# Two streams for a step's preparation in a single-core RWKV-7 and short-convolution layer

## The chip, the cores and the metric

The kernel runs on one core of a Trainium2 chip. The metric is the device time of one execution in microseconds; the time given for a kernel is the median of several runs. The profile shows one execution.

## What is computed

One layer of a hybrid encoder on 1024 prompt tokens (one sequence) and 128 sample tokens (8 sequences of 16), D_MODEL 1024, 16 heads of 64. In short:

```python
h = rmsnorm(x, g_norm)
proj = h @ w_in                       # [r, k, v, w_lr, a_lr, z_a | B, C, xb, z_b | g_a, g_b]
pa_mix = pa + mu_shift * (pa_prev - pa)
r, k, v, w_lr, a_lr, z_a = split(pa_mix)
w = exp(-DECAY_SCALE * sigmoid(w_decay0 + tanh(w_lr) @ w_decay2))
a = sigmoid(w_iclr0 + a_lr @ w_iclr2)
kt = k * (1 + (a - 1) * k_replace)
kh = (k * k_removal) / norm(k * k_removal)            # per head
# per token: S = S*diag(w) - (S kh)(a*kh)^T + v kt^T ;  y = S r
o_a = (groupnorm(y) + sum(r * kt * r_bonus) * v) * silu(z_a)
out_b = (B * conv3(C * xb) * silu(z_b)) @ w_o_b
x = x + (sigmoid(g_a) * (o_a @ w_o_a) + sigmoid(g_b) * out_b) @ w_out
x = x + sigmoid(rmsnorm(x, g_ple) @ w_ple_gate) * (p @ w_ple)
y = rmsnorm(x, g_final)
```

## The kernel before, in words

The features lie on the 128 partitions, the tokens along the free dimension. A projection of one 128-column tile of w_in over a block of n tokens is 8 x 3 = 24 matmuls with float16 high and low parts (`dense_parts`, line 162); it accumulates in one of the two PSUM buffers of the pool psd. The tokens go in three blocks: 512 prompt tokens, the 128 sample tokens, the other 512 prompt tokens (BLOCKS, line 22).

The recurrence is done in 24 **steps**: 8 pairs of heads (j) times the three blocks (g); i counts them. A step passes through generators, called streams:

- `prep` (line 364): the decay and the learning rate (`decay`, line 376: products lod and loa, a scan, exponentials), then in one loop the projections of k, r, v and z (TensorE's dk, dr, dv, dz), each mixed with the token before (`mixed`, line 221). After r come the norm of the keys (product pss, a reciprocal square root on VectorE, the broadcast rnb on ScalarE), after v the transposes prn and the scaled keys, after z its tanh (thz) and silu. Ahead of v it waits until the tail of step i-3 is done (line 411), as v and z have three buffers. Temporary tiles come from a pool of seven slots ("ta", TA on line 241).
- `keys` (line 466), the end of prep: the scaled keys and receptances ar and kb. It waits until the step before has transposed its kb (line 470), and at first until all three openings are done.
- `scores` (line 496, psc), `values` (line 525: pk, pv, psb, x), `inverse` (line 568: itt, ig, i, ie, if), a triangular inverse by doubling.
- `chain` (line 656): the recurrence over chunks of 64 tokens, one after another, 8 chunks in a 512-token step and 2 in the sample step; products c and u, state sbd.
- `tail` (line 710): the output y, its group norm on VectorE, transposes py, and the gating with z.

Beside them run `opening` (line 300: normalised input of a block and the low-rank input projection), `conv` (line 781: the four projections C, x, zb and B of the convolution branch for 8 tiles) and `gates_b` (line 832), which computes up to six tiles of the merge gates early (EARLY, line 209: gates b0 to b3, a6 and a7) and stores them in memory (gb_d).

The order of TensorE's work is written out when the program is built, by `go` (line 916), with a clock of modelled TensorE time. A `yield` of a number says how much modelled time the next part needs until its inputs are there. What is ready and no projection goes first, in the order of the list of streams (line 903). Otherwise the next three matmuls of a projection are issued: one that has begun goes on to its end, else a new one begins, the convolution's first where it is behind its pace (its share of its work against the share of chunks done), else by the order of the list:

```python
            fills = more or [x for x in live if x.next == DENSE]
            if fills:
                behind = S_conv.cost / CONV_US < (chunks[0] + LEAD) / 144
                fills.sort(key=lambda x: (x is S_conv) != behind)
                fills[0].step()
```

The table `may` (line 905 on) says when a stream may take its next step. The early gates start when the convolution is done, and none starts when all tails are done (line 913). Weights come in over SP's queue (`load_q`, line 334), in the third step of a pair those of the next pair, and are split by ScalarE and VectorE. The other engines' order is set by a planner from priorities and data.

After the steps the kernel computes the gates that were not early, the two output projections (ob, oa), the merge and w_out (oc), and the per-layer input embedding (pg, ple) with the norms.

Of the kernel before, what the change touches and what calls it, by code (L numbers as in the profile page):

```python
# [23 lines left out]
RN = 512  # L24
# [47 lines left out]
def _build(nc, tc, I, O, top):  # L72
# [40 lines left out]
    def P(n, i):  # L113
        o, w = PN[n]
        return par[:, o + i:o + i + 1]
# [102 lines left out]
    def tt(pool, tag, nm, bufs, n=RBUF):  # L218
        return pool.tile([128, n], F32, tag=tag, name=nm, bufs=bufs)
# [21 lines left out]
    TA = 7  # L241
# [86 lines left out]
    def pair(j):  # L328
        if j not in pairs:
            pairs[j] = s = St()  # L330
            s.w, s.lora = {}, False
        return pairs[j]

    def load_q(j, q):
        s = pair(j)
        if q not in s.w:
            t = {"k": T_K, "r": T_R, "v": T_V, "z": T_ZA}[q]
            s.w[q] = load_w(I["w_in"][t + j], f"p{j}_{t}")
# [25 lines left out]
    def prep(f):  # L364

        j, g = f.j, f.g
        f.s = s = pair(j)
        load_lora(j)
        if g == 0:
            s.sst = wk.tile([128, 8, 64], F32, tag="sst", name=f"sst{j}", bufs=1)  # L370
            SP.dma_start(s.sst, I["wkv"][j])
        blk = o, n = f.blk
        smp, nch, npr, nm = f.smp, f.nch, f.npr, f.nm
        sl, ns = (16, 8) if smp else (64, nch)

        def decay():
            th = []
            yield lambda: f.i or S_open.at > 0
            for q, hb in (("d", 0), ("a", 1)):
                yield 2.0 * hb  # L380
                ps = psa.tile([128, 512], F32, tag="a", name="lo" + q + nm)
                lr = (lrd, lra)[hb]
                mm(ps[:, :n], s.lwh[:, hb, :], lr[:, o:o + n], start=True, stop=False)
                mm(ps[:, :n], s.lwl[:, hb, :], lr[:, o:o + n], start=False, stop=True)
                t = tt(st_, "ta", "th" + q + nm, TA)[:, :n]
                A.activation(t, ps[:, :n], AF.Tanh, scale=0.5 * IWS, bias=half[:, hb, j:j + 1])
                th.append(t)
            thd, tha = th
            G.tensor_scalar(out=thd, in0=thd, scalar1=1.0, scalar2=None, op0=ALU.add)
            cum = tt(st_, "ta", "cum" + nm, TA)[:, :n]  # L390
            V.tensor_tensor_scan(out=cum, data0=(scan_s if smp else scan_p), data1=thd, initial=0.0,
                                 op0=ALU.mult, op1=ALU.add)
            pb = tt(st_, "ta", "pb" + nm, TA)[:, :ns * (sl + 1)].rearrange("p (c t) -> p c t", t=sl + 1)
            G.memset(pb[:, :, 0:1], 1.0)
            seg = lambda x: x.rearrange("p (c t) -> p c t", t=sl)
            A.activation(pb[:, :, 1:], seg(cum), AF.Exp, scale=-0.5 * CDEC)
            pt = small.tile([128, 8], F32, tag="pt", name="pt" + nm, bufs=4)
            G.tensor_copy(pt.unsqueeze(2)[:, :ns, :], pb[:, :, sl:sl + 1])
            pi = tt(st_, "ta", "pi" + nm, TA)[:, :n]
            A.activation(pi, cum, AF.Exp, scale=0.5 * CDEC)  # L400
            return tha, pb, pt, pi

        if f.i:
            tha, pb, pt, pi = yield from decay()

        m = {}
        ahead = g == 2 and j + 1 < 8
        for q, t in (("k", T_K), ("r", T_R), ("v", T_V), ("z", T_ZA)):
            load_q(j, q)
            if q == "v":  # L410
                yield lambda: S_tail.at >= f.i - 2
            ps = yield from dense_parts(s.w[q], blk, q + nm)
            if ahead:
                load_q(j + 1, q)
            if q == "v":
                x = f.v = tt(wk, "v", "v" + nm, 3, RN)[:, :n]
            elif q == "z":
                x = f.zs = tt(wk, "zs", "zs" + nm, 3, RN)[:, :n]
            else:
                x = tt(st_, "ta", q + nm, TA)[:, :n]  # L420
            mu = (zmu[:, i, j:j + 1] for i in range(3)) if q == "z" else (
                P("mu", t + j), mum[:, t + j:t + j + 1], mus[:, t + j:t + j + 1])
            mixed(ps, t + j, blk, x, *mu, q + nm)
            m[q] = x
            if q == "k" and not f.i:
                f.k_done = True
                tha, pb, pt, pi = yield from decay()
            if q == "r":
                x = m["k"]
                yield 4.0  # L430

                sq = tt(st_, "ta", "sq" + nm, TA)[:, :n]
                A.activation(sq, x, AF.Square, scale=P("krem", j))
                pss = psa.tile([128, 512], F32, tag="a", name="pss" + nm)
                for i in range(npr):
                    mm(pss[:, 2 * i:2 * i + 2], sq[:, i * 128:(i + 1) * 128], onesb[:, 0:128:64], start=True, stop=True)
                ssm = small.tile([128, 8], F32, tag="ssm", name="ssm" + nm)
                V.tensor_scalar(out=ssm[:, :2 * npr], in0=pss[:, :2 * npr], scalar1=1e-24, scalar2=None, op0=ALU.max)
                rn = rsqrt(ssm[:, :2 * npr], 2 * npr, "k%d" % npr)
                rnb = tt(st_, "ta", "rnb" + nm, TA)[:, :n]  # L440
                A.activation(rnb.rearrange("p (q t) -> p q t", t=64), rn.unsqueeze(2).to_broadcast([128, 2 * npr, 64]),
                             AF.Copy)
            if q == "v":

                k = m["k"]
                yield 3.0
                prn = psa.tile([128, 512], F32, tag="a", name="prn" + nm)
                for i in range(npr):
                    tr(prn[:, i * 128:(i + 1) * 128], rnb[:, i * 128:(i + 1) * 128], ident)
                kt = tt(st_, "ta", "kt" + nm, TA)[:, :n]  # L450
                V.tensor_scalar(out=kt, in0=tha, scalar1=half[:, 2, j:j + 1], scalar2=half[:, 3, j:j + 1],
                                op0=ALU.mult, op1=ALU.add)
                V.tensor_tensor(out=kt, in0=kt, in1=k, op=ALU.mult)
                V.scalar_tensor_tensor(out=k, in0=k, scalar=P("krem", j), in1=prn[:, :n], op0=ALU.mult, op1=ALU.mult)
                V.scalar_tensor_tensor(out=tha, in0=tha, scalar=1.0, in1=k, op0=ALU.add, op1=ALU.mult)
        if ahead:
            load_lora(j + 1)
        z = m["z"]

        thz = tt(st_, "ta", "thz" + nm, TA)[:, :n]  # L460
        A.activation(thz, z, AF.Tanh)
        V.scalar_tensor_tensor(out=f.zs, in0=thz, scalar=1.0, in1=z, op0=ALU.add, op1=ALU.mult)
        f.pt = pt
        yield from keys(f, m["k"], kt, tha, m["r"], pb, pi)

    def keys(f, kh, kt, b2, r, pb, pi):
        j = f.j
# [375 lines left out]
    steps = []  # L843
# [27 lines left out]
    class Stream:  # L871
# [28 lines left out]
        def fill(self):  # L900
            return self.next in (DENSE, MORE)

    S_chain, S_tail, S_val, S_inv, S_scores, S_open, S_prep, S_conv, S_gate = every = [
        Stream(k) for k in (chain, tail, values, inverse, scores, opening, prep, conv, gates_b)]
    may = {S_chain: lambda i: S_inv.at > i and S_val.at > i and S_tail.at >= i - 1,
           S_tail: lambda i: S_chain.at > i,
           S_val: lambda i: S_scores.at > i and S_chain.at >= i - 1 and (i < 2 or steps[i - 2].y_done),
           S_inv: lambda i: S_scores.at > i,
           S_scores: lambda i: S_prep.at > i and (i < 3 or steps[i - 3].y_done),
           S_prep: lambda i: S_chain.at >= i - 3 and S_open.at >= (0, 2, 3)[min(i, 2)],  # L910
# [31 lines left out]
    rk.close()  # L942


    ow = top.enter_context(tc.tile_pool(name="ow", bufs=1, side="right"))
    mr = top.enter_context(tc.tile_pool(name="mr", bufs=1, side="right"))
    oo = top.enter_context(tc.tile_pool(name="oo", bufs=1))
# [44 lines left out]

    obs = []
    for j in range(KT):
        if T_GB + j not in EARLY:
            gate(ms[j], T_GB + j, f"b{j}")
            for k in range(2 * (j - 4), 2 * (j - 3)):
                obs.append(load_o(ob_d, k, f"b{k}"))
    for j in range(KT):
        if T_GB + j in EARLY:  # L1000
            SP.dma_start(ms[j], gb_d[EARLY.index(T_GB + j)])
        w = load_wr(I["w_ob"][j], f"b{j}")
        for blk in BL3:
            o, n = blk
            ps = dense_r(w, obs, blk, f"ob{j}_{o}")
            V.scalar_tensor_tensor(out=ms[j][:, o:o + n], in0=ms[j][:, o:o + n], scalar=1.0, in1=ps,
                                   op0=ALU.add, op1=ALU.mult)
# [2 lines left out]

    def gate_a(j):
        gts[j] = op.tile([128, NTOK], F32, tag="gt", name=f"gt{j}", bufs=2)
        if T_GA + j in EARLY:
            SP.dma_start(gts[j], gb_d[EARLY.index(T_GA + j)])
        else:
            gate(gts[j], T_GA + j, f"a{j}")

# [229 lines left out]
```

## Time and profile before

| | |
|---|---|
| median of 3 runs | 1896.75 us (1890.45 to 1900.36) |
| the profiled execution | 1898.31 us, span 1895.6 us |
| TensorE (PE) busy | 1800.8 us, 95% |
| VectorE (DVE) busy | 1250.8 us, 66% |
| ScalarE (ACT) busy | 813.6 us, 43% |
| GpSimd (POOL) busy | 215.7 us, 11% |
| mean share of the DMA queue for data | 17.6% |

The span runs from the first instruction to the last; what the device time has beyond it lies around the program. Matmul names begin with the tile that they write: dk is the projection of the keys, c and u are the chain's products. PEld are weight loads, which overlap PE. A line such as L92 is that of a helper through which all matmuls go, so the groups are told apart by their tiles.

### The profile page before, as it was taken

The numbers are of one execution on the slowest core, as the hardware profiler recorded it, in microseconds if no ns is written. First come the engines' busy times: TensorE is split into PE (matmuls) and PEld (weight loads), VectorE is DVE, ScalarE is ACT, GpSimd is POOL, SyncE is SP. The second block draws the span as 40 slices with busy tenths as digits, with TensorE's granted clock in tenths as the row PEclk, the third lists the DMA queues.
The fourth block names the chain that finished last, engine by engine and source line by source line (L and its number), as shares of the span: only waits on it lengthen the run. The fifth ranks groups of instructions, "written<-read, shape, count | busy, mean of one in ns | idle before, by whom it ended". The sixth has DMA issues, their size and how long they took to land.

```text
span 1895.6 us, 37827 instructions
## 1 busy us (share of the span) xinstructions
PE 1800.8 (95%) x15374; PEld 1247.8 (66%) x15374; DVE 1250.8 (66%) x3183; ACT 813.6 (43%) x1865; POOL 215.7 (11%) x333
## 2 busy tenths in 40 slices
PE   5999999999999999999999999999899999999997
PEld 2555665565666666566566556565499678999766
DVE  5577887788688788788788778861422411545765
ACT  6454563554545545446446446442401311333321
POOL 1001121111111111111111102000000011300000
PEclk9999999999999999999999999999999999999999
DMA  6011102001111101101101100212512410242012
GB/s 222 12 34 49 53 17 75 29 25 54 36 42 44 47 31 49 53 31 36 63 31 35 64 30 25 78 65 86 164 46 67 132 43 22 97 149 74 10 44 72
DMA packets 45486, 110.65 MB, mean 58 GB/s; under 512 B 6400, under 2 KB 21632, under 8 KB 45312
## 3 DMA queue, kind: packets, MB, share of 16 engines
q1 hardware_dynamic: 45312, 108.24, 17.6%
q8 instruction: 120, 1.97, 0.4%
q14 instruction: 54, 0.44, 0.1%
HBM read 87.94 MB, written 20.28 MB: 57 GB/s over the span
## 4 chain that ended last, share of the span: by engine, by line
PE 66%; DVE 20%; ACT 7%; DMA 3%; issue 3%; POOL 1%; POOLq 0%; SPq 0%; DVEq 0%; ACTq 0%
PE ob L92 5%; PE oc L92 5%; PE oa L92 5%; PE dr L92 4%; PE dgb L92 4%; PE dz L92 4%; PE pg L92 4%; PE dga L92 4%; PE dk L92 3%; PE dB L92 3%; PE dzb L92 3%; PE dv L92 3%; PE u L92 2%; PE dC L92 2%; PE dx L92 2%
## 5 line engine op out<-in xcount | busy, mean ns | idle before, releaser
L92 PEld LDWEIGHTS <-whip 128*128 128x128 f16 x1536 | 132.6, 99 | 72.1 <-issue 6.5
L686 POOL TENSOR_SCALAR Spt<-sbd,pt 128x128 f32<-128x128 f32 x128 | 91.0, 711 | 612.4 <-DVE sbd L705 611.5
L705 DVE SCALAR_TENSOR_TENSOR sbd<-u,pt,Spt 64x64 f32<-64x64 f32 x256 | 71.9, 281 | 69.0 <-PE u L92 66.0
L92 PEld LDWEIGHTS <-wlop 128*128 128x128 f16 x768 | 75.5, 98 | 61.8 <-issue 2.2
L92 PE MATMUL dgb<-hx,whigb 128*128 128x512 f16 (+1 forms) x480 | 110.4, 326 | 4.2 <-ACT ms L991 3.4
L626 ACT ACTIVATE bdgt<-ig 64x512 f16<-64x512 f32 (+1 forms) x208 | 106.6, 512 | 2.7
L92 PE MATMUL dB<-hx,whiB 128*128 128x512 f16 (+1 forms) x384 | 90.6, 331 | 4.4 <-ACT sho L232 4.4
L92 PE MATMUL dx<-hx,whiX 128*128 128x512 f16 (+1 forms) x384 | 90.1, 328 | 2.8 <-ACT sho L239 2.8
L92 PE MATMUL dC<-hx,whiC 128*128 128x512 f16 (+1 forms) x384 | 90.1, 329 | 2.1 <-ACT sho L232 2.1
L92 PE MATMUL dzb<-hx,whiZ 128*128 128x512 f16 (+1 forms) x384 | 88.1, 326 | 3.4 <-ACT sho L232 1.7
L92 PE MATMUL dv<-hx,whip 128*128 128x512 f16 (+1 forms) x384 | 90.2, 330 | 0.9 <-DVE zb L828 0.9
L92 PE MATMUL dz<-hx,whip 128*128 128x512 f16 (+1 forms) x384 | 90.6, 329 | 0.0
L92 PE MATMUL dr<-hx,whip 128*128 128x512 f16 (+1 forms) x384 | 90.1, 330 | 0.0
L693 ACT ACTIVATE yst<-c 64x128 f32<-64x128 f32 x144 | 38.8, 270 | 119.4 <-DVE xs L692 117.6
L92 PE MATMUL pg<-xn,pg 128*128 128x384 f16 (+1 forms) x576 | 88.5, 309 | 0.0
L92 PE MATMUL dk<-hx,whip 128*128 128x512 f16 (+1 forms) x384 | 88.2, 326 | 0.0
L92 PEld LDWEIGHTS <-pg 128*128 128x128 f16 x768 | 65.5, 98 | 26.9 <-issue 2.1
L619 ACT ACTIVATE gt<-ig 128x512 f16<-128x512 f32 (+1 forms) x104 | 54.2, 521 | 67.2 <-PE ig L92 66.7
L627 DVE CAST_PREDICATED tt<-cph,i 128x512 f16<-128x512 uint16 (+1 forms) x104 | 61.8, 594 | 29.9 <-PE i L92 26.0
L699 ACT ACTIVATE vu<-u 64x64 f32<-64x64 f32 x288 | 62.4, 217 | 39.8 <-PE u L92 36.3
L92 PE MATMUL dgb<-hx,wlogb 128*128 128x512 f16 (+1 forms) x240 | 74.4, 326 | 0.0
L92 PE MATMUL oc<-mh,wohc 128*128 128x384 f32 x192 | 64.9, 338 | 3.7 <-DVE ms L1075 3.7
(327 smaller groups left out, 4875.8 us busy)
## 6 DMA issues: line engine op xcount, KB each, us to landing
wstp<-i_w_in SPq DMA_DIRECT2D x32, 512.0 KB, 3.5
wstgb<-i_w_in SPq DMA_DIRECT2D x10, 512.0 KB, 3.5
xt<-i_x SPq DMA_DIRECT2D x9, 512.0 KB, 6.1
ob_d<-zb SPq DMA_DIRECT2D x8, 576.0 KB, 2.9
ostb<-ob_d SPq DMA_DIRECT2D x24, 192.0 KB, 2.5
osta<-oa_d SPq DMA_DIRECT2D x24, 192.0 KB, 2.4
xr<-i_xT SPq DMA_DIRECT2D x8, 576.0 KB, 3.6
wstC<-i_w_in SPq DMA_DIRECT2D x8, 512.0 KB, 3.6
```

Source lines behind the costliest of these rows:

```text
L92: PE.matmul(out, lhsT, rhs, start=start, stop=stop)
L619: A.activation(Gt, pg, AF.Copy, scale=-1.0)
L626: A.activation(Gb[R, :, R], pg[R], AF.Copy, scale=-1.0)
L627: V.copy_predicated(out=Tt, mask=bc(lvt[:, b, :]).bitcast(U16), data=p1)
L686: G.tensor_scalar(out=Spt, in0=S, scalar1=pt[:, c:c + 1], scalar2=None, op0=ALU.mult)
L693: A.activation(yst[Vh, p, :], pc[Vh, 0:128], AF.Copy)
L699: A.activation(vu[Uh, c, H], pu[H, H], AF.Copy, scale=-1.0)
L705: V.scalar_tensor_tensor(out=S2[H, H], in0=pu[H, 128 + h * 64:192 + h * 64], scalar=pt[H, c:c + 1], in1=Spt[H, H], op0=ALU.mult, op1=ALU.add)
```

## The change

The loop over k, r, v and z in `prep` becomes a loop over k and r. A new function `project` holds the body of the loop, and a new stream `prep_v` projects v and z and computes the tanh and silu of z. The new stream S_pv stands in the list ahead of S_prep. It may take step i when the tail of step i-3 is done and the opening of its block is; `values` waits for it. The transposes prn now come after a modelled 6.0 us, counted from the issue of the norm, where a modelled 3.0 us behind the projection of v stood. The gates that were stored early are no longer a fixed six, but those that the stream got done, at least four; the others are computed in the last stage.

```diff
-        ahead = g == 2 and j + 1 < 8
-        for q, t in (("k", T_K), ("r", T_R), ("v", T_V), ("z", T_ZA)):
-            load_q(j, q)
-            if q == "v":
-                yield lambda: S_tail.at >= f.i - 2
-            ps = yield from dense_parts(s.w[q], blk, q + nm)
-            if ahead:
-                load_q(j + 1, q)
...
-            mixed(ps, t + j, blk, x, *mu, q + nm)
-            m[q] = x
+        for q in "kr":
+            x = m[q] = yield from project(f, q)
             if q == "k" and not f.i:
                 f.k_done = True
                 tha, pb, pt, pi = yield from decay()
...
-            if q == "v":
 
                 k = m["k"]
-                yield 3.0
+                yield 6.0
                 prn = psa.tile([128, 512], F32, tag="a", name="prn" + nm)
...
-        if ahead:
+        if g == 2 and j + 1 < 8:
             load_lora(j + 1)
-        z = m["z"]
-
-        thz = tt(st_, "ta", "thz" + nm, TA)[:, :n]
+        f.pt = pt
+        yield from keys(f, m["k"], kt, tha, m["r"], pb, pi)
+
+    def project(f, q):
+
+        j, nm, blk = f.j, f.nm, f.blk
+        s = pair(j)
+        t = {"k": T_K, "r": T_R, "v": T_V, "z": T_ZA}[q]
+        load_q(j, q)
+        ps = yield from dense_parts(s.w[q], blk, q + nm)
+        if f.g == 2 and j + 1 < 8:
+            load_q(j + 1, q)
...
+        mixed(ps, t + j, blk, x, *mu, q + nm)
+        return x
+
+    def prep_v(f):
+
+        f.v = yield from project(f, "v")
+        z = f.zs = yield from project(f, "z")
+        thz = tt(st_, "ta", "thz" + f.nm, TA)[:, :f.blk[1]]
         A.activation(thz, z, AF.Tanh)
         V.scalar_tensor_tensor(out=f.zs, in0=thz, scalar=1.0, in1=z, op0=ALU.add, op1=ALU.mult)
-        f.pt = pt
-        yield from keys(f, m["k"], kt, tha, m["r"], pb, pi)
...
-    S_chain, S_tail, S_val, S_inv, S_scores, S_open, S_prep, S_conv, S_gate = every = [
-        Stream(k) for k in (chain, tail, values, inverse, scores, opening, prep, conv, gates_b)]
+    S_chain, S_tail, S_val, S_inv, S_scores, S_open, S_pv, S_prep, S_conv, S_gate = every = [
+        Stream(k) for k in (chain, tail, values, inverse, scores, opening, prep_v, prep, conv, gates_b)]
...
-           S_val: lambda i: S_scores.at > i and S_chain.at >= i - 1 and (i < 2 or steps[i - 2].y_done),
+           S_pv: lambda i: S_tail.at >= i - 2 and S_open.at >= (1, 2, 3)[min(i, 2)],
+           S_val: lambda i: S_scores.at > i and S_pv.at > i and S_chain.at >= i - 1 and (i < 2 or steps[i - 2].y_done),
...
+    early = EARLY[:S_gate.at]
+    assert len(early) >= 4
...
-        if T_GA + j in EARLY:
-            SP.dma_start(gts[j], gb_d[EARLY.index(T_GA + j)])
+        if T_GA + j in early:
+            SP.dma_start(gts[j], gb_d[early.index(T_GA + j)])
```

## Rows read from the trace of the kernel before

**Rows 1.** The page: its span, its first part, and one line of its sixth.

```profile
span 1895.6 us, 37827 instructions
...
PE 1800.8 (95%) x15374; PEld 1247.8 (66%) x15374; DVE 1250.8 (66%) x3183; ACT 813.6 (43%) x1865; POOL 215.7 (11%) x333
...
wstp<-i_w_in SPq DMA_DIRECT2D x32, 512.0 KB, 3.5
```

**Rows 2.** Stretches: from:to, length, then busy (instructions) per engine, clock, DMA.

```profile
0.00:150.00 150.00, 118.54 (x918) 69.12 (x918) 91.87 (x226) 82.57 (x157) 13.37 (x33) 0.95 0.26 89
150.00:1345.00 1195.00, 1153.57 (x11133) 728.99 (x11133) 926.19 (x2465) 590.89 (x1438) 170.66 (x276) 1.00 0.15 47
600.00:1050.00 450.00, 435.94 (x4304) 278.31 (x4303) 370.75 (x997) 236.07 (x576) 66.85 (x113) 1.00 0.13 42
```

**Rows 3.** The chain that ended last, around 320 us: start, us, what.

```profile
316.51 3.74 PE dB L92 x9
...
321.02 1.94 PE dB L92 x9
```

**Rows 4.** TensorE's timeline, steady part: start, us, operation [idle before, releaser].

```profile
631.26 1.10 PE L92 MATMUL psc<-ar,kb 64*64 64x128 f32 x32
...
660.44 0.33 PE L96 MATMUL c<-ident,xa 128*128 128x128 f32 x1
...
685.75 0.38 PE L92 MATMUL c<-sbd,ar 128*128 128x128 f32 x2
...
777.11 0.38 PE L92 MATMUL dz<-hx,wlop 128*128 128x512 f16 x1
...
778.72 1.10 PE L92 MATMUL psc<-ar,kb 64*64 64x128 f32 x32
```

**Rows 5.** The chain that ended last, a gate in the last stage.

```profile
1510.08 11.71 PE dga L92 x72
```

**Rows 6.** TensorE's waits, 150 to 1340 us: in total, times, longest.

```profile
PE py L96 <- DVE yc L760: 6.1, 10, 2.4
PE c L92 <- DVE sbd L705: 4.6, 8, 0.8
PE dB L92 <- ACT sho L232: 4.4, 2, 2.3
...
PE psb L92 <- DVE yc L749: 1.7, 2, 1.2
```

**Rows 7.** Timelines of TensorE and ScalarE, from r's last product to rnb, two steps.

```profile
658.02 0.38 PE L92 MATMUL dr<-hx,wlop 128*128 128x512 f16 x1
662.95 1.03 PE L92 MATMUL pss<-cpk,sq 128*128 128x2 f32 x8
669.42 0.63 ACT L441 ACTIVATE rnb<-nrk 128x512 f32<-128x512 f32 x1 [0.85 <-DVE nrk L139]
...
745.99 1.05 PE L92 MATMUL pss<-cpk,sq 128*128 128x2 f32 x8 [0.27 <-ACT vu L550]
757.87 0.63 ACT L441 ACTIVATE rnb<-nrk 128x512 f32<-128x512 f32 x1 [2.75 <-DVE nrk L139]
```

**Rows 8.** TensorE's timeline: three waits of a projection for an eviction.

```profile
112.28 1.01 PE L92 MATMUL dx<-hx,whiX 128*128 128x512 f16 x2 [2.53 <-ACT sho L239]
...
253.03 0.59 PE L92 MATMUL dx<-hx,whiX 128*128 128x512 f16 x2 [0.28 <-ACT sho L239]
...
316.51 0.75 PE L92 MATMUL dB<-hx,whiB 128*128 128x512 f16 x2 [2.30 <-ACT sho L232]
```

**Rows 9.** TensorE's timeline at the start.

```profile
45.83 0.59 PE L92 MATMUL lod<-lrd,lwh 128*128 128x512 f16 x1 [4.36 <-DVE lrd L297]
...
53.98 0.38 PE L92 MATMUL dr<-hx,wlop 128*128 128x512 f16 x1
...
83.83 0.38 PE L92 MATMUL dl<-hx,wlol 128*128 128x512 f16 x1
...
85.55 1.10 PE L92 MATMUL psc<-ar,kb 64*64 64x128 f32 x32
```

More of the change, by code (lines that the diff above doesn't have):

```diff
@@ L406, in prep @@
         m = {}
-        ahead = g == 2 and j + 1 < 8
-        for q, t in (("k", T_K), ("r", T_R), ("v", T_V), ("z", T_ZA)):
-            load_q(j, q)
-            if q == "v":
-                yield lambda: S_tail.at >= f.i - 2
-            ps = yield from dense_parts(s.w[q], blk, q + nm)
-            if ahead:
-                load_q(j + 1, q)
-            if q == "v":
[L416 to L422, printed above, removed]
-            mixed(ps, t + j, blk, x, *mu, q + nm)
-            m[q] = x
+        for q in "kr":
+            x = m[q] = yield from project(f, q)
             if q == "k" and not f.i:
@@ L442, in prep @@
                              AF.Copy)
-            if q == "v":
                 k = m["k"]
-                yield 3.0
+                yield 6.0
                 prn = psa.tile([128, 512], F32, tag="a", name="prn" + nm)
@@ L455, in prep @@
                 V.scalar_tensor_tensor(out=tha, in0=tha, scalar=1.0, in1=k, op0=ALU.add, op1=ALU.mult)
-        if ahead:
+        if g == 2 and j + 1 < 8:
             load_lora(j + 1)
-        z = m["z"]
-        thz = tt(st_, "ta", "thz" + nm, TA)[:, :n]
+        f.pt = pt
[8 more added lines that the diff above has]
+            load_q(j + 1, q)
+        if q in "vz":
+            x = tt(wk, "v" if q == "v" else "zs", ("v" if q == "v" else "zs") + nm, 3, RN)[:, :blk[1]]
+        else:
+            x = tt(st_, "ta", q + nm, TA)[:, :blk[1]]
+        mu = (zmu[:, i, j:j + 1] for i in range(3)) if q == "z" else (
+            P("mu", t + j), mum[:, t + j:t + j + 1], mus[:, t + j:t + j + 1])
+        mixed(ps, t + j, blk, x, *mu, q + nm)
[4 more added lines that the diff above has]
+        thz = tt(st_, "ta", "thz" + f.nm, TA)[:, :f.blk[1]]
         A.activation(thz, z, AF.Tanh)
         V.scalar_tensor_tensor(out=f.zs, in0=thz, scalar=1.0, in1=z, op0=ALU.add, op1=ALU.mult)
-        f.pt = pt
-        yield from keys(f, m["k"], kt, tha, m["r"], pb, pi)
     def keys(f, kh, kt, b2, r, pb, pi):
@@ L994, in _build @@
     for j in range(KT):
-        if T_GB + j not in EARLY:
+        if T_GB + j not in early:
             gate(ms[j], T_GB + j, f"b{j}")
@@ L999, in _build @@
     for j in range(KT):
-        if T_GB + j in EARLY:
-            SP.dma_start(ms[j], gb_d[EARLY.index(T_GB + j)])
+        if T_GB + j in early:
+            SP.dma_start(ms[j], gb_d[early.index(T_GB + j)])
         w = load_wr(I["w_ob"][j], f"b{j}")
```

## The prediction

> **What bounds the kernel.** I read the page's first part, then the busy times of a few stretches, then what TensorE waited for, and only then single instructions. TensorE is busy 1800.8 of 1895.6 us [rows 1]. The stretches tell where the other 95 us lie [rows 2]: 150 - 118.5 = 31.5 us before 150 us, 1195 - 1153.6 = 41.4 us in the long middle, where the 24 steps run, and some 22 us behind it, where nothing is changed. VectorE is next: in the steady part (600 to 1050 us) it is busy 370.75 of 450 us, 82%, against 435.94 us, 97%, of TensorE.
>
> A busy share need not mean that TensorE works at its rate. Here it does: nine matmuls of 512 columns take 1.94 us, 216 ns each, and that is 512 columns at 2.4 GHz (213 ns) [rows 3]. So a microsecond is won only where TensorE idles, or where its clock falls. The Trainium skill ("Perfetto Trace Analysis", Identifying the Most-Contended Engine) says that matmul occupancy is a poor measure of headroom and that the share of weight loads is a better one. By that rule the 66% of weight loading would leave a third of the time to be won; the 216 ns speak against it, and I forecast by them (rival C is the rule's case).
>
> What the change aims at is there, too. The steps repeat every 778.72 - 631.26 = 147.5 us (three steps, one pair of heads) [rows 4]. At 777.11 us the last matmul of the gate's projection is issued, and 1.6 us later the scores of the same step: the scores do wait for the values' and the gate's projection. The recurrence stands still meanwhile: the sample step's last chunk starts at 660.44, the next step's first at 685.75, which is 25.3 us; the next step's scores (631.26) come late, and its inverse with them [rows 4]. But TensorE doesn't stand still in this gap. It fills it with the convolution's and later the early gates' products. Per period it works 435.94 / (450 / 147.5) = 142.9 us and idles 4.6.
>
> **The parts, and what each costs.**
>
> *The scores come earlier.* In a 512-token step k, r, the norm and its transposes are no longer followed by two projections ahead of the keys. The chain gets shorter by up to 25.3 us a pair, but the work that filled the gap (convolution, two of the six early gates) has still to be done, after the recurrence instead of beside it. A gate costs 11.71 us in the last stage [rows 5], 72 matmuls as before, and the code of the change lets the number of early gates fall. I cost this at 0: TensorE pays the same matmuls in another order. If the cover were gone (no fill left beside a chain that waits), up to 25.3 us a pair would come back as idle time; there are six gates and the convolution as fill, and the change only frees more of it. The store and reload of a gate that is no longer early go with it; they lie on SP's queue beside dense work: 0.
>
> *Waits that go.* Of the 41.4 us in the middle, 6.1 + 1.7 us are TensorE waiting behind the tail's group norm on VectorE (py, psb), 4.6 us for the state update (c) [rows 6]. In the steps where the norm of the keys and the tail's norm fall together, both rsqrt chains share VectorE. When the preparation is no longer held by the values' wait for the tail, the two should move apart; that is an assumption, as the place of either in time is not to be read off this trace. I take the 7.8 us of py and psb as gone and leave the state update. Bounds: 0 to 7.8 + 4.6 = 12.4 us.
>
> *The reciprocal norm's transposes (prn) come earlier.* Before them stood the product of the values (24 matmuls of 216 ns, 5.2 us) and a modelled 3.0 us; now a modelled 6.0 us alone. A modelled 4.0 us came out as 662.95 - 658.02 = 4.9 us (last r product to pss) [rows 7], so I expect about 6.9. What has to be ready is rnb: pss starts at 662.95 and takes 1.03, rnb ends at 669.42 + 0.63, 6.1 us later, which just fits. In the third step of the pair pss ends at 747.04 and rnb at 758.50, 11.5 us later, with the tail's norm on VectorE in between [rows 7]. TensorE runs in order, so a late rnb holds everything behind it: chunks, inverse and products. Bounds: 0, and 8 x (11.5 - 6.9) = 37 us if every third step stays so. As the collision is what I expect to go, I take 2 us.
>
> *A seventh buffer.* While the norm is computed, the pool of staging tiles (7) holds tha, pb, pi, k, r, sq and rnb; the gate's tanh (thz) now may want an eighth slot at that moment and waits, or rnb waits for it. Before, the gate came last. The tanh is on ScalarE (43% busy [rows 1]), and nothing of the recurrence needs it: 0, its upper end lies within the 37 us above.
>
> *Two short tiles in a row.* For the sample step v and z are now one after the other (128 columns, a quarter of 5.2 us each), and so are k and r, on two PSUM buffers; the third tile waits for the first one's eviction. Such runs in the trace cost 2.53 and 0.28 us [rows 8]. Eight sample steps: 0 to 8 x 2.53 = 20 us; the steady one is the later one, so 8 x 0.28 = 2.2 us.
>
> *The start.* The product for r of the first step moves behind v and z, as the new stream stands ahead of the old one where both could begin a product: 2 x 5.2 us later. The first scores (85.55 us) come 1.7 us behind the last product of the third opening (83.83 us) [rows 9], which the keys wait for in any case; r was through by 54 us [rows 9], so some 10 us later still fits. 0. The 4.36 us wait for the first decay product [rows 9] stays, as that product is issued first.
>
> *Weights.* The loads for v and z of the next pair move to the new stream, still behind their last use; SP's queue lands one in 3.5 us [rows 1], and among TensorE's longest waits in the middle none is for a weight [rows 6]. 0.
>
> Sum: -7.8 + 2 + 2.2 = -3.6 us. The profiled execution took 1898.3 us (span 1895.6), 1.6 us above the median of 1896.75. So 1898.3 - 3.6 = 1894.7, and against the median 1893.
>
> **The rivals.** A measurement of this kernel can tell some 0.5%, 9.5 us, from no change.
>
> A, slower: rnb stays late. VectorE is 82% busy and the same work is packed into a shorter stage. The place is prn, and the point from which it decides is rnb later than 6.9 us after pss. The price of a late one is 4.6 us, and more, since TensorE is slower for a while after such a wait: behind one of 2.30 us nine matmuls took 3.74 us in place of 1.94 [rows 3, 8], 1.8 us lost. Eight steps: 8 x (4.6 + 1.8) = 51 us, 1948 in full; with half of the steps hit, 1922. For it: the 11.5 us. Against: that one is a collision of two norms, and the change moves one of them. Chance 0.27.
>
> B, faster: the stalls thin out beyond py and psb. The state update's 4.6 us and the waits of the convolution's products for an eviction (dB, 4.4 us [rows 6]) come from bunches on VectorE and ScalarE, and steps that overlap more evenly have fewer: -7.8 - 4.6 - 4.4 = -16.8 us, 1880. Chance 0.29.
>
> C, much faster: TensorE has slack after all, and every gap's 25.3 us is won: 8 x 25.3 = 202 us, 1695. The 97% speak against it. Chance 0.02.
>
> D, it doesn't do what it says: the values' stream comes first in the list, so wherever both could begin a product v and z still go ahead of k and r; the scores stay where they are, and the time is 1897. Chance 0.14.
>
> **How the numbers follow.** My own case 0.28 (1893, within 0.5%), D 0.14: same 0.42. B and C: faster 0.31. A: slower 0.27. The range goes from 1873, 7 us below B's 1880 (the smaller waits that I left alone can go too), to 1920, just short of A's half case: C's 0.02 and some 0.04 of B lie below it, and about 0.14 above, A's upper half.
>
> **What would show it.** Right: scores of a 512-token step within some 15 us of its r product and without the gate's last matmul just ahead; the 25.3 us gap at half or less; fewer than six gates stored early; TensorE's idle time in the middle near 38 us. A: waits of prn for ScalarE's rnb of several us, with slower matmuls behind them. B: 25 us of idle time or less. Wrong altogether: another number of matmuls in the middle stage than the moved gates explain, or idle time that appears behind 1345 us, in a stage that I left alone.

## The result, and the profile after

The changed kernel takes 1961.87 us (median of 4 runs, 1958.81 to 1964.17); the kernel before took 1898.55 beside it. The ratio is 1.0346, 95% interval 1.0326 to 1.0365: 63 us slower. I had forecast 1893, with a range up to 1920.

The page of the changed kernel, its span, its first part and one line of its sixth:

```profile
span 1956.9 us, 37875 instructions
...
PE 1816.4 (93%) x15374; PEld 1260.4 (64%) x15374; DVE 1251.0 (64%) x3183; ACT 815.3 (42%) x1865; POOL 234.5 (12%) x333
...
gb_d<-gb SPq DMA_DIRECT2D x6, 576.0 KB, 2.8
```

The same 15374 matmuls as in [rows 1]. The span is 61.3 us longer. TensorE idles 1956.9 - 1816.4 = 140.5 us in place of 94.8, which is 45.7 us, and its busy time has grown by 15.6 us for the same work. VectorE and ScalarE do what they did before. Six gates are stored early, as before, not fewer.

Where it idles, in the stretches of [rows 2] (150 to 1345 us and the steady part among them):

```profile
0.00:150.00 150.00, 116.82 (x894) 68.19 (x895) 92.39 (x225) 82.74 (x157) 12.04 (x31) 0.97 0.26 90
150.00:1345.00 1195.00, 1107.59 (x10740) 706.10 (x10739) 911.56 (x2429) 578.33 (x1406) 188.82 (x275) 0.98 0.13 41
1345.00:1957.00 612.00, 591.96 (x3744) 486.13 (x3742) 247.03 (x529) 154.25 (x303) 33.61 (x28) 0.99 0.25 78
600.00:1050.00 450.00, 416.70 (x4097) 265.30 (x4096) 349.83 (x909) 222.23 (x536) 71.89 (x105) 0.99 0.13 40
```

Start and end are as they were (33.2 and 20.0 us idle). The middle has 87.4 us of idle time in place of 41.4, and its granted clock is 0.98 in place of 1.00. The longer busy time fits that: 15.6 us are 0.9% of 1800.8, and the mean granted clock of the span fell by 0.8%, from 0.991 to 0.983. In the steady part VectorE is *less* busy than before, 350 of 450 us. So no engine has become the bound by its load.

What TensorE waited for, over the whole run (the longest lines of the new kinds, in total us, times, longest):

```profile
PE prn L96 <- ACT rnb L425: 7.6, 3, 4.1
PE if L92 <- DVE scy L525: 6.9, 4, 3.5
...
PE psc L92 <- DVE ar L488: 4.7, 4, 2.6
PE dx L92 <- ACT sho L232: 4.7, 2, 2.5
PE dr L92 <- ACT sho L232: 4.5, 2, 2.9
...
PE pss L92 <- ACT sq L417: 4.2, 4, 2.3
PE pS L92 <- POOL vux L737: 4.0, 2, 2.3
...
PE psc L92 <- DVE ar L482: 3.2, 4, 1.2
...
PE psc L92 <- DVE bdgt L650: 2.9, 3, 2.5
PE psc L92 <- DVE kb L493: 2.7, 4, 2.2
```

In [rows 6] the longest were the tail's py and the chain's c, a few us each. Now the scores (psc) wait for the keys (ar, kb), the transposes prn for the norm, the inverse (if) for the masks of the scores (scy), the projections for evictions (sho). Summed by tile up to the last tail, psc stands for 19.7 us where it stood for 4.8, the projections together for 25.9 in place of 14.7.

One step of the changed kernel shows why, TensorE's and then VectorE's timeline from prn to the scores:

```profile
646.35 0.60 PE L96 MATMUL prn<-ident,rnb 128*128 128x128 f32 x4
...
649.73 0.44 PE L92 MATMUL psc<-ar,kb 64*64 64x128 f32 x4 [0.43 <-DVE ar L488]
```

```profile
646.98 0.75 DVE L437 SCALAR_TENSOR_TENSOR k<-k,par,prn 128x512 f32<-128x512 f32 x1 [0.50 <-PE prn L96]
647.76 0.69 DVE L438 SCALAR_TENSOR_TENSOR tha<-tha,k 128x512 f32<-128x512 f32 x1
...
648.98 0.69 DVE L488 TENSOR_TENSOR ar<-k,pb 128x512 f32<-128x512 f32 x1
649.59 0.68 DVE L493 SCALAR_TENSOR_TENSOR kb<-tha,pi 128x512 f32<-128x512 f32 x1
```

Between prn and the scores VectorE has to do these four operations, 2.8 us of busy time together, and whatever else stands in its queue. The plan allows 1.0 us for it. In the kernel before that was enough, as TensorE's prn and VectorE's last operation on the keys of one step show:

```profile
769.07 0.63 PE L96 MATMUL prn<-ident,rnb 128*128 128x128 f32 x4
```

```profile
774.08 0.69 DVE L489 SCALAR_TENSOR_TENSOR kb<-tha,pi 128x512 f32<-128x512 f32 x1
```

The last keys were ready 5.7 us behind prn. The projection of z lay between prn and the scores, and these came at 778.72 [rows 4], 9.65 us behind. Before the change that is so in every step: the projection of z lies between, and the scores come 9.6 us or more behind prn. In the changed kernel they come 3.4 us behind in the step shown, and under 5 us in 8 of the 24 steps, with no whole projection between. At the scores of these eight TensorE stands for some 11 of psc's 19.7 us. Where VectorE is behind, one late operand follows another:

```profile
452.75 1.11 PE L96 MATMUL prn<-ident,rnb 128*128 128x128 f32 x4 [4.06 <-ACT rnb L425]
...
459.73 0.44 PE L92 MATMUL psc<-ar,kb 64*64 64x128 f32 x4 [1.05 <-DVE kb L492]
...
463.75 0.20 PE L92 MATMUL ie<-tt,bdmh 128*128 128x64 f16 x1 [0.93 <-DVE scy L525]
...
472.42 0.29 PE L92 MATMUL if<-tn,bdgt 128*128 128x64 f16 x2 [3.47 <-DVE scy L525]
```

That is 9.5 us of waits in 24; from 450 to 500 us the granted clock was 0.90. The first of them is the collision that the prediction saw before the change: VectorE works on the reciprocal square roots of the keys (nrk) and of the tail (nry) in turn, and rnb ends 12.3 us behind pss:

```profile
439.41 1.03 PE L92 MATMUL pss<-cpk,sq 128*128 128x2 f32 x8
```

```profile
448.68 0.16 DVE L139 SCALAR_TENSOR_TENSOR nry<-nay,nry 128x8 f32<-128x8 f32 x1
...
449.03 0.15 DVE L139 SCALAR_TENSOR_TENSOR nrk<-nak,nrk 128x8 f32<-128x8 f32 x1
```

```profile
452.07 0.63 ACT L425 ACTIVATE rnb<-nrk 128x512 f32<-128x512 f32 x1 [1.34 <-DVE nrk L139]
```

The chain, TensorE's timeline (last chunks of sample steps, first of other steps):

```profile
658.61 0.27 PE L96 MATMUL c<-ident,xa 128*128 128x128 f32 x1
...
706.53 0.38 PE L92 MATMUL c<-sbd,ar 128*128 128x128 f32 x2
...
915.02 0.49 PE L92 MATMUL c<-sbd,ar 128*128 128x128 f32 x2
...
986.50 0.33 PE L96 MATMUL c<-ident,xa 128*128 128x128 f32 x1
...
994.67 0.49 PE L92 MATMUL c<-sbd,ar 128*128 128x128 f32 x2
...
1057.41 0.49 PE L92 MATMUL c<-sbd,ar 128*128 128x128 f32 x2
```

The gap that stood at 25.3 us in nearly every pair is now 8.2 us here (986.50 to 994.67) and 47.9 there (658.61 to 706.53). Even the pair with the short gap takes 1057.41 - 915.02 = 142.4 us, 5.1 us less than the 147.5 before and about what TensorE had to do in such a period (142.9). Its chunks take longer instead: the last of the first chain starts 56.1 us behind the first, where it was 50.0; as I read it, they wait for their turn on TensorE. So the aim was met in some steps, and there was little to win by it.

### The profile page after: what moved, and what is told of

Read it like the earlier page. It is cut to its first block, busy times and chain, and to the rows that moved or that the text cites. A ratio compares the mean times of both kernels' runs of the same rounds, so it can differ in the third digit from the quotient of the medians.

```text
span 1956.9 us, 37875 instructions
## 1 busy us (share of the span) xinstructions
PE 1816.4 (93%) x15374; PEld 1260.4 (64%) x15374; DVE 1251.0 (64%) x3183; ACT 815.3 (42%) x1865; POOL 234.5 (12%) x333
## 4 chain that ended last, share of the span: by engine, by line
PE 67%; DVE 21%; ACT 6%; issue 3%; DMA 2%; POOLq 0%; POOL 0%; SPq 0%; DVEq 0%; ACTq 0%
PE ob L92 5%; PE dgb L92 5%; PE oc L92 5%; PE dr L92 5%; PE oa L92 4%; PE dC L92 4%; PE pg L92 4%; PE dga L92 4%; PE dz L92 3%; PE dk L92 3%; PE dv L92 3%; PE dB L92 3%; PE u L92 2%; PE dzb L92 2%; PE dx L92 2%
## 5 line engine op out<-in xcount | busy, mean ns | idle before, releaser
L690 POOL TENSOR_SCALAR Spt<-sbd,pt 128x128 f32<-128x128 f32 x128 | 96.2, 752 | 615.2 <-DVE sbd L709 614.3
L631 DVE CAST_PREDICATED tt<-cph,i 128x512 f16<-128x512 uint16 (+1 forms) x104 | 61.9, 596 | 35.0 <-PE i L92 33.5
L637 DVE CAST_PREDICATED tn<-cph,i 128x512 f16<-128x512 uint16 (+1 forms) x104 | 61.6, 593 | 17.0 <-PE i L92 16.0
```

The lines of the kernel that those rows point to most:

```text
L631: V.copy_predicated(out=Tt, mask=bc(lvt[:, b, :]).bitcast(U16), data=p1)
L637: V.copy_predicated(out=Tn, mask=bc(lv[:, b, :]).bitcast(U16), data=p2)
L690: G.tensor_scalar(out=Spt, in0=S, scalar1=pt[:, c:c + 1], scalar2=None, op0=ALU.mult)
```

## The experiments

Theory 1 is that early scores have lost their cover, that is the work between the keys and the scores in which VectorE made the operands. Theory 2 is the order: the values' stream, first in the list, takes TensorE ahead of k and r. Each difference below is against the changed kernel, unless it says otherwise; times are medians of 2 to 4 runs, ratios against the kernel before on the same chip.

**A longer wait ahead of the scores.**

```diff
-            yield 1.0, 2
+            yield (1.0 if p0 else 5.0), 2
```

> Edit: the modelled wait ahead of a step's first scores is 5.0 us in place of 1.0; the rest is the changed kernel. Theory 1 (lost cover: the scores are issued before VectorE has made the keys, and TensorE stands): TensorE's waits at psc, 18.3 us in the middle stage, fall below 5, those at if, ie and itt behind them (10.6 us together) by half, and the time falls by 18 to 30 us, to 1932 to 1944 us. Theory 2 (order: the values' stream, first in the list, takes TensorE ahead of k and r): the waits only move to other tiles, and the time stays within 8 us of 1962.

1964.66 us, ratio 1.0354 (1.0301 to 1.0408). psc fell from 19.7 to 11.1 us, and if, ie and itt from 10.8 to 7.5, but the time didn't: py rose from 4.5 to 12.3 and the projections from 25.9 to 36.7. A miss for theory 1 in this form; the time is where theory 2 had it.

**The same, and a longer wait ahead of prn.**

```diff
-                yield 6.0
+                yield 9.0
```

> Edit: as the run before, and the modelled wait ahead of the transposes prn is 9.0 us in place of 6.0. Theory 1: prn's 7.6 us and the slow stretches behind its long waits go too, 8 to 14 us below the run before. Theory 2: within 8 us of 1962.

1944.67, ratio 1.0249 (1.0159 to 1.0340). prn fell from 7.6 to 0.8 us, psc to 6.1, and 17 us were won, though the two runs lie 12 us apart (1938.57 and 1950.76); the projections stand at 38.7 us, lod at 13.7.

**The order of the list.**

```diff
-    S_chain, S_tail, S_val, S_inv, S_scores, S_open, S_pv, S_prep, S_conv, S_gate = every = [
-        Stream(k) for k in (chain, tail, values, inverse, scores, opening, prep_v, prep, conv, gates_b)]
+    S_chain, S_tail, S_val, S_inv, S_scores, S_open, S_prep, S_pv, S_conv, S_gate = every = [
+        Stream(k) for k in (chain, tail, values, inverse, scores, opening, prep, prep_v, conv, gates_b)]
```

> Edit: the values' stream stands behind the preparation in the list of streams, not ahead of it; the modelled waits are those of the changed kernel. Theory 1: the keys come no later after the norm than before, so psc, prn and what waits behind them stay at 25 us or more, and the time stays above 1940 us. Theory 2: k and r come first, the gaps between the chains (48 us where 25 stood) close to under 25, the waits for evictions (dx, dr, dz: 12 us) go, and the time falls to 1895 to 1925 us.

1967.89, ratio 1.0372 (1.0302 to 1.0441): no better. In this kernel's list of waits two lines now stand ahead:

```profile
PE dzb L92 <- ACT sho L232: 15.9, 4, 4.5
...
PE prn L96 <- ACT rnb L425: 12.9, 6, 3.4
```

psc is down to 3.9 us by the order alone, with the scores 7.9 us or more behind prn in every step, and the loss is the same. Theory 2 falls as the explanation of the time; and lost cover at the scores cannot be all of it either, for here the scores have their cover.

**All three.** 

> Edit: all three together: the values' stream behind the preparation, 5.0 us ahead of the scores, 9.0 us ahead of prn. Theory 1: about the same as the run with both waits, within 10 us. Theory 2: about the same as the run with the order alone, within 10 us. If both causes carry a share, this is the lowest of the four, 1890 to 1910 us.

1944.41, ratio 1.0248 (1.0198 to 1.0298): the run with both waits again. So far the idle time moves from tile to tile; up to the last tail the sums are 119.6, 113.0, 122.2 and 109.2 us in these four, 119.0 in the changed kernel and 69.9 before. Theory 3 was that the evictions of two streams of projections are at fault, theory 4 that TensorE outruns the other engines wherever it can.

**A modelled eviction.** On the run with both waits; lod also 2.5 us later.

```diff
-            fills = more or [x for x in live if x.next == DENSE]
+            fills = more or [x for x in live if x.next == DENSE and min(dbank) <= pe[0]]
...
+        dbank[slot] = pe[0] + 3.0
```

> Edit: on the run with both waits, a new projection may only begin when the modelled eviction of the last but one (3.0 us after its end) is over, and the first decay product is issued 2.5 us later. Theory 3 (the streams send more projections and evictions in a row than ScalarE and VectorE can clear, and TensorE stands at the PSUM buffers): the waits at the projections (38.7 us with both waits, 13.5 before) and at lod (13.7 against 4.4) fall to 20 us together, and the time falls from 1945 to 1905 to 1925 us. Theory 4 (TensorE is ahead of the other engines altogether, whichever tile it waits at): the idle time only moves to other tiles, and the time stays within 10 us of 1945.

1948.79, ratio 1.0260 (1.0219 to 1.0301): within 10 us. The projections still wait 29.6 us; lod fell to 4.8, psb rose to 10.4. Theory 3 falls in this form.

**One stream after the other.** On the run with both waits.

```diff
-           S_pv: lambda i: S_tail.at >= i - 2 and S_open.at >= (1, 2, 3)[min(i, 2)],
+           S_pv: lambda i: S_prep.at > i and S_tail.at >= i - 2 and S_open.at >= (1, 2, 3)[min(i, 2)],
...
-           S_prep: lambda i: S_chain.at >= i - 3 and S_open.at >= (0, 2, 3)[min(i, 2)],
+           S_prep: lambda i: S_pv.at >= i and S_chain.at >= i - 3 and S_open.at >= (0, 2, 3)[min(i, 2)],
```

> Edit: on the run with both waits, the two streams take turns: v and z of a step only when its k, r and keys are done, and the next step's k and r only behind them, so that the order is k, r, keys, v, z in single file. Theory 3: with one stream of mixed projections the waits at the projections and lod go back to some 25 us, and the time to 1900 to 1920 us. Theory 4 (the early scores themselves are what VectorE cannot follow): 1935 us or more.

1926.74, ratio 1.0144 (1.0109 to 1.0179), 18 us better than with two streams and between the two expectations. The projections are back at 13.8 us, as before the change, and every pair looks like the next. One wait stands out, once a pair:

```profile
PE py L96 <- DVE yc L764: 24.4, 7, 4.8
```

**Shorter norms, in both kernels.**

```diff
-        for _ in range(3):
+        for _ in range(1):
```

> Edit: the changed kernel with one Newton iteration in place of three in every reciprocal square root (the other two are left out), which takes six short instructions of VectorE from each of the 48 norms of the steps; the order on TensorE is that of the changed kernel. If VectorE's lateness is what TensorE stands for (theories 1, 3 and 4), the time falls by 15 to 35 us, to 1927 to 1947. If the loss lies in the order on TensorE itself (theory 2), it falls by under 8 us.

> Edit: the same omission in the kernel before. Its TensorE idles 41 us in the middle stage, and waits at py, psb and pss, where a norm is awaited, are some 9 us: 5 to 12 us faster than before, 1885 to 1893 us. If VectorE's lateness is what the change makes worse, the gap between the two light kernels is clearly under the 63 us of the full ones (under 50); else it stays.

The changed kernel gained 26 us (1935.46, ratio 1.0190, 1.0160 to 1.0220), the kernel before 24 us (1874.95, ratio 0.9871, 0.9843 to 0.9900). Lateness of VectorE costs both of them alike, far more than I expected of the second; the gap stays, 60.5 us. So the length of VectorE's norms is not what makes the change dearer.

**Longer waits all over.** The chain's are left alone. In the changed kernel the wait ahead of a step's first scores is also 3.5 us in place of 1.0, 5.25 with the factor. The kernel before has the factor alone.

```diff
-            self.ready = pe[0] + (x if isinstance(x, float) else 0.0)
+            self.ready = pe[0] + (x * (1.0 if self.kind is chain else 1.5) if isinstance(x, float) else 0.0)
```

> Edit: the changed kernel with every modelled wait 1.5 times as long but those of the chain (prn 9.0, tail 16.5, the inverse's stages likewise) and 5.25 us ahead of the scores. Theory 5 (the modelled waits had been fitted to the old order; in the new one they are too short all over, so products are issued that VectorE and ScalarE cannot have ready): the idle time of the stage of the steps falls from 119 to 80 us or less and the time to 1890 to 1920 us. Theory 4 (with the scores early, TensorE outruns the other engines, whatever is modelled): still 1935 us or more.

> Edit: the same factor of 1.5 in the kernel before. Theory 5: there the waits fit, and only the 6 us of py and a few others can go: 1885 to 1900 us. If this kernel gains as much as the changed one does by the same factor, the factor tells nothing about the change.

2017.67 and 2015.42, both ratios about 1.06, and the second is far outside what was expected. They tell nothing about the change: with these waits the gap in the chain is over 50 us in the one and around 43 in the other, in most pairs, the stage gets longer than the work that could fill it, and TensorE runs dry at the end of it. Its busy tenths in the first of the two:

```profile
PE   5999999999999999999899878888989999999997
```

**The scores put back behind the values and the gate.** The two streams and all waits stay.

```diff
-           S_scores: lambda i: S_prep.at > i and (i < 3 or steps[i - 3].y_done),
+           S_scores: lambda i: S_prep.at > i and S_pv.at > i and (i < 3 or steps[i - 3].y_done),
```

> Edit: the changed kernel, but a step's scores wait until its values' stream is done too, which puts back what the change took away; the two streams stay. Theory 1 (lost cover): with the projections of v and z between the keys and the scores the waits at psc fall from 19.7 to under 8 us, and the time to under 1930 us. Theory 2 or 4: the time stays within 12 us of 1962, as v and z are often done before the keys in any case.

1927.29, ratio 1.0145 (1.0116 to 1.0174): 35 us of the 63 are back by this one condition. psc is at 4.0 us, below the kernel before. What is left in its list of waits:

```profile
PE prn L96 <- ACT rnb L425: 5.7, 6, 1.9
PE dk L92 <- ACT sho L239: 5.3, 2, 2.9
PE lod L92 <- DVE k L437: 5.1, 1, 5.1
```

**Single file, and a longer wait of the tail.**

```diff
-        yield 11.0
+        yield 16.0
```

> Edit: on the single-file order, the tail's modelled wait ahead of py is 16.0 us in place of 11.0. In that run py is the largest wait, 24.4 us in seven waits of some 3.5 us, one a pair. If the modelled waits are what is wrong there (theory 5), they go, and the time falls from 1927 by 20 to 30 us, to 1897 to 1907. If not, they turn up at another tile, and it stays above 1917.

1908.73, ratio 1.0052 (1.0028 to 1.0075). py's 24.4 us are gone; 18 us were won, 2 less than the lower end of what was expected. Of the versions with two streams this one loses least, 9 us, though its scores do not wait for v and z. In every step they come 5.5 us or more behind prn, and in 22 of the 24 most of the projection of v stands between:

```profile
850.18 0.60 PE L96 MATMUL prn<-ident,rnb 128*128 128x128 f32 x4
...
852.13 0.59 PE L92 MATMUL dv<-hx,whip 128*128 128x512 f16 x2
...
857.44 1.10 PE L92 MATMUL psc<-ar,kb 64*64 64x128 f32 x32
```

psc stands for 7.2 us in all. The gap between the chains is back too, at 20 us or more in every pair.

**The scores put back, and prn and lod waited for.** On the run with the scores put back.

```diff
-                yield 6.0
+                yield 9.0
...
-                yield 2.0 * hb
+                yield 2.0 * hb if hb or not f.i else 4.0
```

> Edit: on the run with the scores behind the values (1927 us), 9.0 us in place of 6.0 ahead of prn and 4.0 us ahead of the first decay product lod. In that run prn and lod hold 6.3 + 9.6 us of waits that the kernel before has not. If these two are the rest of the loss, the waits go and the time falls to 1898 to 1912 us. If TensorE merely meets the lateness elsewhere, it stays above 1918.

1912.37, ratio 1.0084 (1.0063 to 1.0105): prn has no wait left, lod 5.0 us, and 15 us more are back, just short of what was expected if these two were all the rest. The gap between the chains is 20.8 us in nearly every pair.

**The same two waits with the scores early.** 

> Edit: the same two waits in the changed kernel, the scores early as it has them. If the early scores are the larger share, as the run with the scores put back says (35 us), this one stays 25 to 40 us above the run before it, at 1930 to 1950 us. If prn and lod are the larger share, it comes below 1920.

1992.78, ratio 1.0495 (1.0474 to 1.0515), worse than the changed kernel and 80 us above the run before it, from which it differs by the one condition on the scores. In its waits the scores' operands lead:

```profile
PE psc L92 <- DVE ar L488: 14.9, 7, 3.3
PE psc L92 <- DVE kb L492: 6.8, 2, 4.3
```

psc stands for 39.3 us in all, where the run before it has 5.8. The direction was as expected, the size twice that. In the profiled executions TensorE idles 155.7 us here and 116.3 in the run before it, and its busy time is 1831.6 against 1798.3 us at a mean granted clock of 0.975 against 0.992: 39.4 us of waits and 33.3 us of slower work.

**A version that beats both.** The kernel before with two Newton iterations in place of three. 

> Edit: the kernel before with two Newton iterations in place of three in every reciprocal square root; the last one is left out. With one iteration it was 24 us faster than the kernel before; each iteration is three short instructions of VectorE per norm, so about half of it: 1883 to 1892 us.

1885.06, ratio 0.9936 (0.9913 to 0.9959), as expected. It has nothing of the change in it; with one iteration it was 1874.95.

## Why the prediction was wrong

*What bounds the kernel* held. TensorE had next to no slack: a gap closed from 25.3 to 8.2 us brought a period of 142.4 us, about its own work. Rival C is out. The Trainium skill ("Perfetto Trace Analysis", Identifying the Most-Contended Engine) names MFU and the busy share of weight loads as measures of headroom. The second does not agree with this trace: weight loads were busy for 66% of the span before, and the closed gap won 5.1 us in its pair. The first was not worked out here.

*"The scores come earlier ... I cost this at 0"* is the step that failed. It asked what would fill TensorE when the recurrence is done sooner, and not what lay between the keys and the scores. The projections of v and z were not only in the way: v's lay between the norm and prn, and z's covered VectorE's work on the keys, for which the plan allows 1.0 us. I had in [rows 4] the scores 1.6 us behind the gate's last matmul and read it as a delay that goes; it was also the cover, and I priced no term for what is late next. In its place the runs showed this: holding the scores back behind v and z gave 35 us in the changed kernel, and with longer waits at prn and lod 80 us (1992.78 to 1912.37). psc alone is 39.3 - 5.8 = 33.5 us of the 39.4 us of idle time between these two; the other 33.3 us are slower work. The single-file run with the longer wait of the tail has the projection of v between prn and the scores, and lost 9 us in place of 63.

Two things limit this. With the order of the list turned round the scores had their cover, psc stood for 3.9 us, and the time was 1967.89: the cover is not enough where two streams make other operands late (prn 12.9, lod 13.3, the projections 41.8 us). And in both runs that lost least the recurrence's gap is also back, at 20 us or more. How much of the loss comes from missing cover at the scores, and how much from a preparation packed closer beside the recurrence, no run separates.

*prn, 2 us out of 0 to 37.* It had 7.6 us in three waits, the longest 4.1. Within the bounds. Mending prn together with lod gave 15 us with the scores put back, and cost 31 us with the scores early (1992.78). The collision of norms that I expected to go did not go in every step: it made the longest of the three waits.

*A seventh buffer, 0.* In that longest wait rnb was held by nrk on VectorE, not by a buffer.

*Waits that go, -7.8 us.* py and psb, which I had counted as gone, stand at 4.5 + 4.6 = 9.1 us. Nothing went; the assumption on which it stood, that the two norms move apart, was not in the trace, as I had said.

*Two short tiles in a row, 2.2 us.* The projections' waits together rose by 11 us, in the variants with two streams by up to 27. In the single-file run they are back at 13.8 us, so they come with two streams at a time; that these waits add up to time was not shown, since modelling the eviction took 9 us of them away and won nothing.

*Start and weights* cost next to nothing, as said: TensorE idles 33.2 us in place of 31.5 before 150 us, and no listed wait is for a weight.

Rival A had the sign, and an in-order TensorE held by a late operand was the mechanism, but its place was prn and its point rnb. In the changed kernel psc came first, 19.7 us against 7.6. Rival D saw rightly that v and z still go ahead of r in places (between 671 and 685 us, inside the gap of 47.9 us), but the order of the list was worth nothing when it was turned round.

Of the 63 us, then, the condition on the scores gave back 35, and after it the waits of prn and lod 15. The remaining 13 us (1912.37 against 1898.93) are open: in that run the projections wait 25.0 us against 14.7, psb 9.8 against 1.7 and ie 8.4 against 0.3, and no run takes them away one by one. The shares depend on the order in which they are taken, as 35 and 80 us for the same condition show. By the other way, both waits, single file and a longer wait of the tail, 53 us came back (1908.73).

## What to carry to other kernels

Before a projection is moved out of the way of what waits behind it, ask what it covers: a wait that the plan of an in-order engine puts at 1 us may be that short only because a projection (5.2 us here) lay in it. Where the bound engine is 97% busy, as here, a shorter chain behind it has little to win, and a late operand stops the whole engine. And if an idle wait is mended and the time stays, compare the sum of waits, not the one line. Here four mendings left the sum within 109 to 122 us. Putting the scores back lowered it to 95.6, and single file to 94.7, with the longer wait of the tail to 81.8.

## What the runs showed of the hardware beyond that

Waits cost more than their length. The idle time of the changed kernel rose by 45.7 us and its busy time by 15.6 us for the same matmuls; the mean granted clock of TensorE fell from 0.991 to 0.983. In the kernel before, a wait of 2.30 us was followed by nine matmuls in 3.74 us in place of 1.94 [rows 3, 8].

VectorE's short operations weigh on this kernel's time though VectorE is only 66% busy. Two Newton iterations less in the kernel before took 1250.8 - 1206.2 = 44.6 us from VectorE's busy time and 24 us from the kernel's. About half of it is idle time of TensorE (94.8 to 81.9 us), the rest its busy time (1800.8 to 1790.6 us); the granted clock was 0.994 in place of 0.991. I had expected 5 to 12 us, from the waits at py, psb and pss.
